# Layer 0's late modulation on TensorE and by row sums, and a z gate that is kept until the scan is done

## The chip, the cores and the metric

The program runs on one core of one Trainium2 chip, as one launch. The metric is the device time of one execution, in microseconds (us). TensorE does the matmuls, VectorE (DVE) and ScalarE (ACT) the elementwise work, GpSimd (POOL) a part of it, and SyncE (SP) issues nearly all DMA transfers, in one queue. Each engine takes its instructions strictly in the order in which they stand.

## The reference

A backbone of two layers works on 128 context tokens and 512 latent tokens, 640 columns in all, with 1024 features. What matters here:

```
mod = silu(c) @ w_ada[l] + b_ada[l]          # (c_ctx for context, c for latent tokens)
shift1, scale1, gate1, shift2, scale2, gate2 = split(mod, 6)
h = rmsnorm(x) * (1 + scale1) + shift1
cq, ckv, krope, dq, dk, dv, z, xbc, dt_raw = split(h @ w_in)
o_a = latent attention(cq, ckv, krope); o_d = differential attention(dq, dk, dv)
y   = scan(xbc, dt_raw)                      # forward and backward, chunks of 128 tokens
o_c = rmsnorm(y * silu(z), ssm_norm_g)
x  += gate1 * (concat(o_a, o_d, o_c) @ w_out)
h   = rmsnorm(x) * (1 + scale2) + shift2
x  += gate2 * (relu(h @ w_ff1)**2 @ w_ff2)
```

Everything is float32. A modulation vector of 1024 numbers for two conditions is a product of a 1024x1024 block of `w_ada` with two vectors. The blocks are numbered j = 0 to 5 in the order of the split: 0 is the first shift, 2 the first gate, 3 the second shift, 4 the second scale.

## The kernel before, in words

Activations lie with features on partitions: `x[k]` holds 128 features of all 640 tokens, for k = 0 to 7. Large products run as three passes over a high and a low part of each operand (`fm`, L318; `tm_chunk`, L781 to L783). The layer's mixing stage (`mixing`, L594) is written as generators: `projections` (the low-rank and query/key projections, then z in `gate`, L795), `ssd` (the scan), `att_b` (differential attention), `prep_a` (keys and queries of the latent attention), `att_a` (latent attention), `wo_part` (output projection). `weave` (L186) steps whichever part is furthest behind its share, and so sets the order in which the program is written; a scheduler then orders each engine's queue by readiness with that order as priority. The first weave ends when the projections are done, the second when the scan is, the third covers the rest of the differential attention, and two more the latent attention.

A part named `fill` carries modulation vectors that are needed later in the layer or in the next one. `pace` (L1673, L1681, L1691) sets its share in each stage from `FILL`, three numbers a layer. Layer 0's fill before is `ada_all` with blocks 2, 3 and 4: `ada_dve` loads 16 pieces of 256 KB of a block and adds them up, each row weighted with the condition's value, in the tile `wc` (VectorE L433; ScalarE L431 and L436; GpSimd L437), and ends with one-column matmuls against ones (`adad`, L414) that sum over partitions. Layer 1's fill is `ada_rows` with blocks 3 and 4: the condition is broadcast to rows once (`crow`, L463), and each piece of the transposed block is multiplied and summed along its row by one VectorE instruction with an accumulator (`junk`, L484). The first gate has to be ready before the output projection begins, so a loop steps the fill nine times there.

In `gate`, z's tile `zth` holds z times 1 + tanh(z/2). Then the generator yields until the scan's output `ys` of its tokens exists, and multiplies it (L813). The scan's `gated` (L1217) waits for both products of a chunk, normalizes it, and its result is transposed (`yT`) for the output projection. `zth` comes from a ring X of 6 buffers; the ring G has 48, the ring Y 13. `PB` is a ring of 3 PSUM banks, from which small products of all parts are taken.

Of the kernel before, what the change touches and what calls it, by code (L numbers as in the profile page):

```python
# [21 lines left out]
P = 128  # L22
# [77 lines left out]
ADA_T = [(0, 5)] + [(1, j) for j in (1, 0, 2, 3, 4, 5)]  # L100
# [4 lines left out]
def build(nc, tc, a, ctx):  # L105
# [291 lines left out]
    def ada_dve(l, j):  # L397

        def fetch(i):
            qr, k2 = divmod(i, 4)  # L400
            raw = Y([P, 2, 256], name="wa")
            nc.sync.dma_start(raw, a["w_ada"][k2 * 256:(k2 + 1) * 256, j * 1024 + qr * 256:j * 1024 + (qr + 1) * 256]
                              .rearrange("(k p) c -> p k c", p=P))
            return raw

        pt = S([P, 8, 2], "adapt", 2)
        raws = [fetch(0), fetch(1)]

        def columns(qr, acc):
            pp = PB("adad")  # L410
            for m in range(2):
                for v in range(2):
                    c = 2 * m + v
                    pe.matmul(pp[:, c:c + 1], acc[:, v, m * P:(m + 1) * P], ones[:, 0:1], start=True, stop=True)  # L414
            act.copy(out=pt[:, qr * 2:qr * 2 + 2], in_=pp[:, :4].rearrange("p (m v) -> p m v", v=2))

        lag = []
        for i in range(16):
            qr, k2 = divmod(i, 4)
            if k2 == 0:  # L420
                if len(lag) == 2:
                    columns(*lag.pop(0))
                acc = Y([P, 2, 256], name="wc")
                lag.append((qr, acc))
            for kk in range(2):
                k = 2 * k2 + kk
                r = raws[i][:, kk]
                for v in range(2):
                    s_ = sc[:, k, v:v + 1]
                    if k == 0:  # L430
                        act.activation(out=acc[:, v], in_=r, func=AF.Copy, scale=s_)  # L431
                    elif v == 0 or k in ADA_DVE[l]:
                        vec.scalar_tensor_tensor(out=acc[:, v], in0=r, scalar=s_, in1=acc[:, v], op0=ALU.mult, op1=ALU.add)  # L433
                    else:
                        t_ = X([P, 256], name="adat")
                        act.activation(out=t_, in_=r, func=AF.Copy, scale=s_)  # L436
                        pool.tensor_tensor(out=acc[:, v], in0=acc[:, v], in1=t_, op=ALU.add)  # L437
            if i + 2 < 16:
                raws.append(fetch(i + 2))
            if i % 2:  # L440
                yield
        for qa in lag:
            columns(*qa)
        ada_finish(l, j, pt)
        yield

    def ada_all(items):
        for l, j in items:
            for _ in ada_dve(l, j):
                mark("fill")  # L450
                yield
                mark("fill")

    def ada_rows(items):
# [19 lines left out]
        for i, (l, j, m, h) in enumerate(units):  # L474
            if m == 0 and h == 0:
                res = S([P, 2, KD, 2], "adares", 2)
            for v in range(2):
                junk = X([P, 512], name="junk")
                sum_ = res[:, h, m, v:v + 1]
                if 2 * h + v in ROWS_POOL:  # L480
                    pool.tensor_tensor(out=junk, in0=raws[i], in1=row[v][h], op=ALU.mult)
                    act.activation(out=junk, in_=junk, func=AF.Copy, accum_out=sum_)
                else:
                    vec.scalar_tensor_tensor(out=junk, in0=raws[i], scalar=1.0, in1=row[v][h], op0=ALU.mult, op1=ALU.mult,  # L484
                                             accum_out=sum_)
            if i + 2 < len(units):
                raws.append(fetch(i + 2))
            if h == 1:
                if m == KD - 1:
                    sm = S([P, 8, 2], "adapt", 2)  # L490
                    vec.tensor_tensor(out=sm, in0=res[:, 0], in1=res[:, 1], op=ALU.add)
                    ada_finish(l, j, sm)
                yield
                mark("fill")

# [98 lines left out]
    def mixing(l, nrm, fill, late=None, raws={}):  # L594
# [196 lines left out]
        ys, gates = [], [0] * NT  # L791
# [3 lines left out]
        def gate(ci, names, n):  # L795
            lab = f"{l}z"
            for tp, ps in tm_chunk(names, n, lab):
                if tp:
                    m = len(tp)
                    th = X([P, 2, 256], name="zth")  # L800
# [7 lines left out]
                    while len(ys) <= tp[-1]:  # L808
                        yield
                    mark(lab)  # L810
                    for i, t in enumerate(tp):
                        yh = ys[t][:, ci * 256:(ci + 1) * 256]
                        vec.scalar_tensor_tensor(out=yh, in0=yh, scalar=0.5, in1=th[:, i], op0=ALU.mult, op1=ALU.mult)  # L813
                        gates[t] += 1
# [167 lines left out]
        def ssd():  # L982
# [234 lines left out]
            def gated(c):  # L1217
                mark(lab)
                y = ys[c]
                sq = X([P, 512], name="ysq")  # L1220
# [27 lines left out]
            for c in range(NT):  # L1248
                while gates[c] < 2:
                    yield  # L1250
# [432 lines left out]
        while l == 0 and fill.k < 9:  # L1683
# [38 lines left out]
    FILL = (.01, 6, 25), (8, .01, 9)  # L1722
    ROWS_POOL = ()
    ADA_DVE = ((1, 4, 7), (1, 4, 7))
# [303 lines left out]
    for l in range(DEPTH):  # L2028
        f0 = Part(ada_all([(0, 2), (0, 3), (0, 4)]) if l == 0 else ada_rows([(1, 3), (1, 4)]), 1)
# [126 lines left out]
```

## Time and profile before

| | us |
|---|---|
| median of 3 runs (1852.67 to 1854.27) | 1853.48 |
| the profiled execution, device time | 1856.54 |
| its span, first to last instruction | 1854.7 |
| TensorE busy in it | 1734.9 |
| VectorE busy | 1361.3 |
| ScalarE busy | 856.2 |
| GpSimd busy | 499.0 |

The mean granted TensorE clock was 0.946 of full speed. The clock has two levels, 1.2 and 2.4 GHz, so a stretch with a granted clock of 0.75 spent half its time at each. A matmul's busy time contains its way through the array and overlaps with the next one's: how fast matmuls follow each other is read from their starts.

A float32 matmul stands in the trace as two records, each with a weight load of its own; one of the kinds that the large products use stands there as one.

### The profile page before, as it was taken

The page shows a single profiled execution, that of the slowest core. Times are in us where ns is not written, and L with a number is a line of the kernel's source. Part 1 is how long each engine was busy: PE and PEld are TensorE (multiplying, and loading weights), DVE is VectorE, ACT ScalarE, POOL GpSimd, SP SyncE. Part 2 cuts the span into 40 slices and gives each one's busy share as a digit, 9 for nine tenths or more (in the row PEclk, how much of TensorE's full clock was granted, in tenths as well). Part 3 has the DMA queues.
Part 4 walks back from the last instruction along what each step waited for, and adds up shares of the span by engine and source line. Part 5 has one row for each costly group of instructions (what it writes and reads, how often), then busy time and mean ns, then how long its engine had stood idle before and what let it go on. Part 6 is the DMA issues. An engine that isn't in the chain of part 4 may idle for free. (4 is left out here: it accounts for less than half of the span.)

```text
span 1854.7 us, 31728 instructions
## 1 busy us (share of the span) xinstructions
PE 1734.9 (94%) x11572; PEld 1636.7 (88%) x11572; DVE 1361.3 (73%) x2843; ACT 856.2 (46%) x1801; POOL 499.0 (27%) x586
## 2 busy tenths in 40 slices
PE   6999985999899999999998998889999999999998
PEld 4798864888899999999998987668998999999998
DVE  6785768866978988686766769878677887465562
ACT  6553355764555351433544533377544545243240
POOL 1444335212430322304144343331103032130400
PEclk8999976997999999999998998789999999999999
DMA  9121122233343437264441322212423342525341
GB/s 333 56 86 42 49 62 83 80 127 107 109 144 110 141 117 244 89 226 132 164 147 50 98 79 64 70 49 74 137 65 117 94 129 74 187 89 162 112 155 56
DMA packets 116589, 209.01 MB, mean 113 GB/s; under 512 B 13392, under 2 KB 28624, under 8 KB 116432
## 3 DMA queue, kind: packets, MB, share of 16 engines
q1 hardware_dynamic: 115872, 206.80, 34.7%
q8 instruction: 91, 1.49, 0.3%
q14 instruction: 66, 0.54, 0.1%
q10 hardware_dynamic: 560, 0.18, 0.0%
HBM read 179.51 MB, written 27.43 MB: 112 GB/s over the span
## 5 line engine op out<-in xcount | busy, mean ns | idle before, releaser
L1801 ACT CAST wh<-wr 128x512 fp32r<-128x512 f32 x232 | 143.7, 620 | 302.3 <-PE fm L1831 198.0
L1831 PE MATMUL fm<-ul,wh 128*128 128x320 f32 x1024 | 235.2, 311 | 10.2 <-DVE ul L307 10.2
L1802 DVE TENSOR_TENSOR wl<-wr,wh 128x512 fp32r<-128x512 f32 x232 | 180.1, 785 | 77.0 <-issue 41.6
L1831 PE MATMUL fm<-uh,wh 128*128 128x320 f32 x1024 | 234.4, 310 | 1.3 <-DVE x L562 1.3
L1831 PE MATMUL fm<-uh,wl 128*128 128x320 f32 x1024 | 234.5, 310 | 0.0
L1788 POOL TENSOR_TENSOR wS<-wr,wr 128x512 f32<-128x512 f32 x48 | 78.5, 1634 | 494.8 <-DMA wr<-in_W 213.2
L1831 PEld LDWEIGHTS fm<-ul,wh 128*128 128x128 f32 x1024 | 172.1, 189 | 11.3 <-DVE ul L307 11.3
L1831 PEld LDWEIGHTS fm<-uh,wh 128*128 128x128 f32 x1024 | 172.4, 189 | 1.7 <-ACT wh L1801 1.5
L1831 PEld LDWEIGHTS fm<-uh,wl 128*128 128x128 f32 x1024 | 172.7, 189 | 0.0
L484 DVE SCALAR_TENSOR_TENSOR junk<-wa,crow 128x512 f32<-128x512 f32 x224 | 154.0, 735 | 8.4 <-DMA wa<-in_w_adaT 8.2
L562 DVE SCALAR_TENSOR_TENSOR x<-fm,mod,x 128x128 f32<-128x128 f32 (+2 forms) x192 | 72.6, 433 | 108.6 <-PE fm L1831 108.6
L1801 ACT CAST wh<-wS 128x512 fp32r<-128x512 f32 x96 | 59.7, 622 | 142.9 <-PE fm L1831 68.9
L782 PE MATMUL tm<-wl,hhi 128*128 128x256 f32 (+2 forms) x400 | 120.4, 301 | 4.1 <-POOL wl L297 2.0
L781 PE MATMUL tm<-wh,hhi 128*128 128x256 f32 (+2 forms) x400 | 121.2, 303 | 2.5 <-DVE zth L802 1.9
L783 PE MATMUL tm<-wh,hlo 128*128 128x256 f32 (+2 forms) x400 | 120.2, 301 | 0.0
L296 ACT CAST wh<-wr 128x512 fp32r<-128x512 f32 (+2 forms) x108 | 66.5, 625 | 74.8 <-PE fm L318 30.5
L1831 PE MATMUL ffx<-eh,wh 128*128 128x320 f32 x288 | 89.3, 310 | 0.0
L1831 PE MATMUL ffx<-el,wh 128*128 128x320 f32 x288 | 89.2, 310 | 0.0
L1831 PE MATMUL ffx<-eh,wl 128*128 128x320 f32 x288 | 89.1, 309 | 0.0
L782 PEld LDWEIGHTS tm<-wl,hhi 128*128 128x128 f32 x400 | 81.1, 203 | 5.5 <-DVE wl L297 2.7
L781 PEld LDWEIGHTS tm<-wh,hhi 128*128 128x128 f32 x400 | 81.1, 203 | 4.8 <-DVE zth L802 2.6
L783 PEld LDWEIGHTS tm<-wh,hlo 128*128 128x128 f32 x400 | 81.1, 203 | 0.6
(390 smaller groups left out, 4875.8 us busy)
## 6 DMA issues: line engine op xcount, KB each, us to landing
wr<-in_W SPq DMA_DIRECT2D x351, 256.0 KB, 2.8
wa<-in_w_adaT SPq DMA_DIRECT2D x112, 256.0 KB, 4.2
xsave<-x SPq DMA_DIRECT2D x72, 320.0 KB, 2.2
x<-xsave SPq DMA_DIRECT2D x72, 320.0 KB, 5.0
wa<-in_w_ada SPq DMA_DIRECT2D x48, 256.0 KB, 3.6
war<-in_w_ada SPq DMA_DIRECT2D x32, 256.0 KB, 5.3
x<-in_xT SPq DMA_DIRECT2D x16, 320.0 KB, 4.7
out_yT<-x SPq DMA_DIRECT2D x8, 320.0 KB, 2.2
```

The lines of the kernel that those rows point to most:

```text
L296: act.copy(out=hi[:, :w], in_=raw[:, :w])
L484: vec.scalar_tensor_tensor(out=junk, in0=raws[i], scalar=1.0, in1=row[v][h], op0=ALU.mult, op1=ALU.mult, accum_out=sum_)
L562: vec.scalar_tensor_tensor(out=x[m][:, t0:t0 + n], in0=src, scalar=mods[l][:, j, m, v:v + 1], in1=x[m][:, t0:t0 + n], op0=ALU.mult, op1=AL ...
L781: pe.matmul(ps[:, i, :n], hh[k][:, ts], hi[:, c:c + n], start=s, stop=False)
L782: pe.matmul(ps[:, i, :n], hh[k][:, ts], lo[:, c:c + n], start=False, stop=False)
L783: pe.matmul(ps[:, i, :n], hl[k][:, ts], hi[:, c:c + n], start=False, stop=e)
L1788: pool.tensor_tensor(out=box[key], in0=box[x0], in1=box[x1], op=op)
L1801: act.copy(out=hi, in_=raw)
L1802: vec.tensor_tensor(out=lo, in0=raw, in1=f(hi), op=ALU.subtract)
L1831: mm = pe.matmul(o, w_, x_[:, ts], start=s_, stop=e_, skip_group_check=on)
```

## The change

Layer 0's blocks 2 and 3 are made by a new `ada_pe`: for each 128 outputs, a 1024x128 strip of `w_ada` is loaded in two pieces of 256 KB (512 bytes in a row), and eight float32 matmuls of 128x2 accumulate the result directly, with the weights stationary and the condition's two columns moving. Block 4 is made by `ada_rows`, from a transposed copy that is added to the inputs. `FILL` of layer 0 changes, and the loop before the output projection steps the fill until the first gate is made. The z tiles come from the ring G and are kept in a list; `gate` no longer yields for the scan, and `gated` does the products.

```diff
-ADA_T = [(0, 5)] + [(1, j) for j in (1, 0, 2, 3, 4, 5)]
+ADA_T = [(0, 4), (0, 5)] + [(1, j) for j in (1, 0, 2, 3, 4, 5)]
...
+    def ada_pe(l, j):
+
+        def fetch(m):
+            raw = [Y([P, 4, P], name="wa") for _ in range(2)]
+            for h in range(2):
+                c = j * 1024 + m * P
+                nc.sync.dma_start(raw[h], a["w_ada"][h * 512:(h + 1) * 512, c:c + P].rearrange("(k p) c -> p k c", p=P))
+            return raw
+
+        raws = [fetch(0)]
+        res = S([P, KD, 2], "adapt", 2)
+        for m in range(KD):
+            mark("fill")
+            if m + 1 < KD:
+                raws.append(fetch(m + 1))
+            ps = PB("adap")
+            for k in range(KD):
+                pe.matmul(ps[:, 0:2], raws[m][k // 4][:, k % 4], sc[:, k], start=(k == 0), stop=(k == KD - 1))
+            act.copy(out=res[:, m], in_=ps[:, 0:2])
+            if m == KD - 1:
+                ada_finish(l, j, res)
+            yield
+
+    gates_made = []
+
+    def ada_first():
+
+        for m, _ in enumerate(ada_pe(0, 2)):
+            if m == KD - 1:
+                gates_made.append(0)
+            yield
+        yield from ada_pe(0, 3)
+        yield from ada_rows([(0, 4)])
...
-        ys, gates = [], [0] * NT
+        ys, gates = [], [[] for _ in range(NT)]
...
-                    th = X([P, 2, 256], name="zth")
+                    th = G([P, 2, 256], name="zth")
...
-                    while len(ys) <= tp[-1]:
-                        yield
-                    mark(lab)
                     for i, t in enumerate(tp):
-                        yh = ys[t][:, ci * 256:(ci + 1) * 256]
-                        vec.scalar_tensor_tensor(out=yh, in0=yh, scalar=0.5, in1=th[:, i], op0=ALU.mult, op1=ALU.mult)
-                        gates[t] += 1
+                        gates[t].append(th[:, i])
...
             def gated(c):
                 mark(lab)
                 y = ys[c]
+                for ci in range(2):
+                    yh = y[:, ci * 256:(ci + 1) * 256]
+                    vec.scalar_tensor_tensor(out=yh, in0=yh, scalar=0.5, in1=gates[c][ci], op0=ALU.mult, op1=ALU.mult)
...
-                while gates[c] < 2:
+                while len(gates[c]) < 2:
...
-        while l == 0 and fill.k < 9:
+        while not gates_made:
             fill.step()
...
-    FILL = (.01, 6, 25), (8, .01, 9)
+    FILL = (2, 20, 9), (8, .01, 9)
...
-        f0 = Part(ada_all([(0, 2), (0, 3), (0, 4)]) if l == 0 else ada_rows([(1, 3), (1, 4)]), 1)
+        f0 = Part(ada_first() if l == 0 else ada_rows([(1, 3), (1, 4)]), 1)
```

On TensorE, in layer 0's differential attention, before: `stkT` stacks queries and keys, `scB` are scores, `adad` sums `wc` over partitions, `wo` is the output projection.

```order
L318 MATMUL wo_772_3422<-mCl_2864,wh_2834 128x320
L318 MATMUL wo_772_3422<-mCh_2860,wl_2835 128x320
L922 MATMUL stkT_3222<-identr,box_3195 96x128
L414 MATMUL adad_3278<-masksr,wc_3076 128x1
L922 MATMUL stkT_3222<-identr,box_3195 96x128 x3
L1567 MATMUL scB_3399<-stk_3227,stk_3205 128x256
L1567 MATMUL scB_3403<-stk_3227,stk_3205 128x256
L414 MATMUL adad_3278<-masksr,wc_3076 128x1 x3
L414 MATMUL adad_3317<-masksr,wc_3245 128x1 x4
L414 MATMUL adad_3352<-masksr,wc_3284 128x1 x4
```

And now, some fifty rows earlier in the same stage; `kva` are the latent attention's keys and values, and `adap` reads two loaded pieces `wa`:

```order
L1542 MATMUL scB_2966<-stk_2855,stk_2867 128x128
L1303 MATMUL kva_2977<-wukv_2913,ckc_2919 128x512
L456 MATMUL adap_2988<-sc,wa_2634 128x2 x4
L456 MATMUL adap_2988<-sc,wa_2635 128x2 x4
L1303 MATMUL kva_3024<-wukv_2913,cqf_1935 128x512
L1542 MATMUL scB_3033<-stk_2879,stk_2891 128x256
L1542 MATMUL scB_3033<-stk_2901,stk_2891 128x256
L1542 MATMUL scB_3033<-stk_2855,stk_2891 128x128
```

The matmuls that waited for VectorE's sums are gone, and groups of eight that need loaded weights alone stand between the scores from the stage's head on: two such steps lie in the projections before it and fourteen in this stage.

On VectorE, where layer 0's projections end and the differential attention begins (`box` prepares the stacks, `xtm` is the scan's output), before:

```order
L813 SCALAR_TENSOR_TENSOR xtm_1515<-xtm_1515,zth_2791 128x256
L813 SCALAR_TENSOR_TENSOR xtm_1581<-xtm_1581,zth_2791 128x256
L297 TENSOR_TENSOR wl_3810<-wr_3807,wh_3809 128x512
L297 TENSOR_TENSOR wl_4057<-wr_4054,wh_4056 128x512
L1224 TENSOR_SCALAR yvv_2800<-yss_2798 128x1
L1224 TENSOR_SCALAR yvv_2808<-yss_2806 128x1
L802 SCALAR_TENSOR_TENSOR zth_2844<-zth_2844,tm_2813 128x256
L813 SCALAR_TENSOR_TENSOR xtm_1650<-xtm_1650,zth_2844 128x256
L914 TENSOR_TENSOR box_2865<-dxr_2072,box_2865 128x2x32
```

And now:

```order
L1155 TENSOR_TENSOR eg_2740<-eg_2740,cbm_2627 128x512
L886 TENSOR_TENSOR box_2845<-dxr_1455,box_2845 128x2x32 x2
L886 TENSOR_TENSOR box_2857<-dxr_2179,box_2857 128x2x32 x2
L886 TENSOR_TENSOR box_2869<-dxr_1560,box_2869 128x2x32 x2
L1172 TENSOR_TENSOR xtm_1650<-yd_2779,xD_2823 128x512
L886 TENSOR_TENSOR box_2881<-dxr_2283,box_2881 128x2x32
L1186 TENSOR_TENSOR xtm_1650<-xtm_1650,yo_2829 128x256
L1186 TENSOR_TENSOR xtm_1650<-xtm_1650,yo_2836 128x256
```

The end of the scan and the products with z now lie among the first `box` operations instead of ahead of them.

## Rows read from the trace of the kernel before

**Rows 1.** The page: busy time, and the clock in 40 slices.

```profile
PE 1734.9 (94%) x11572; PEld 1636.7 (88%) x11572; DVE 1361.3 (73%) x2843; ACT 856.2 (46%) x1801; POOL 499.0 (27%) x586
...
PEclk8999976997999999999998998789999999999999
```

**Rows 2.** Windows: stretch, length, busy us of PE, PEld, DVE, ACT, POOL, clock, DMA.

```profile
161.00:260.00 99.00, 94.06 (x571) 77.67 (x569) 71.82 (x147) 36.43 (x89) 35.41 (x32) 0.88 0.13 38
...
298.00:325.00 27.00, 15.69 (x80) 14.32 (x80) 22.09 (x46) 11.22 (x29) 12.14 (x17) 0.56 0.24 74
325.00:389.00 64.00, 60.85 (x459) 56.14 (x457) 54.64 (x158) 44.67 (x105) 16.15 (x34) 1.00 0.28 91
389.00:515.00 126.00, 114.44 (x811) 110.17 (x810) 91.42 (x196) 68.78 (x163) 41.80 (x43) 0.89 0.35 112
1089.00:1202.00 113.00, 99.61 (x573) 82.24 (x572) 92.73 (x206) 36.71 (x90) 38.04 (x34) 0.82 0.22 68
1202.00:1240.00 38.00, 30.14 (x157) 23.21 (x157) 27.71 (x80) 27.72 (x68) 14.66 (x36) 0.82 0.11 37
1240.00:1305.00 65.00, 63.40 (x469) 58.23 (x469) 55.98 (x163) 45.71 (x108) 12.84 (x28) 1.00 0.27 86
1305.00:1404.00 99.00, 92.70 (x743) 89.93 (x741) 72.53 (x172) 51.34 (x112) 16.87 (x22) 1.00 0.27 87
```

**Rows 3.** Windows, instructions on tile wc alone, columns as in rows 2.

```profile
260.00:298.00 38.00, 1.35 (x7) 1.32 (x7) 8.11 (x15) 2.70 (x6) 5.77 (x6) 0.68 0.31 99
298.00:325.00 27.00, 6.04 (x26) 5.80 (x26) 15.30 (x26) 0.91 (x2) 8.60 (x10) 0.56 0.24 74
...
389.00:515.00 126.00, 8.77 (x64) 8.85 (x64) 40.19 (x80) 7.25 (x16) 27.65 (x32) 0.89 0.35 112
```

**Rows 4.** Windows, instructions on tile junk alone: DVE busy, clock, DMA.

```profile
1089.00:1202.00 113.00, 22.56 (x56) 0.82 0.22 68
...
1305.00:1404.00 99.00, 18.09 (x56) 1.00 0.27 87
```

**Rows 5.** TensorE's waits (us in total, times, longest): 260:330, then 1089:1205.

```profile
PE adad L414 <- DVE wc L433: 12.5, 3, 8.8
PE stkT L922 <- DVE box L914: 6.9, 3, 3.4
...
PE stkT L922 <- DVE box L914: 5.8, 2, 5.3
...
PE tm L781 <- DVE zth L802: 1.9, 1, 1.9
```

**Rows 6.** Groups by line: count, busy us, mean ns, idle time before and its releaser.

```profile
L484 DVE SCALAR_TENSOR_TENSOR junk<-wa,crow 128x512 f32<-128x512 f32 x224 | 154.0, 735 | 8.4 <-DMA wa<-in_w_adaT 8.2
L433 DVE SCALAR_TENSOR_TENSOR wc<-wa,sc,wc 128x256 f32<-128x256 f32 x120 | 63.6, 566 | 8.7 <-ACT wc L431 7.3 <-POOL wc L437 1.2
L484 DVE DVE_READ_ACCUMULATOR junk<-wa,crow 128x1 f32 x224 | 18.2, 81 | 0.0
L463 PE MATMUL crow<-identr,sc 128*128 128x128 f32 x96 | 11.8, 276 | 0.0
L813 DVE SCALAR_TENSOR_TENSOR xtm<-xtm,zth 128x256 f32<-128x256 f32 x20 | 8.1, 418 | 0.1
```

**Rows 7.** Timeline of TensorE: start, us, line, operation, tiles, records.

```profile
80.89 2.73 PE L700 MATMUL bshp<-mod,wr 128*128 128x2 f32 x24
83.49 0.37 PE L781 MATMUL tm<-wh,hhi 128*128 128x272 f32 x1
```

**Rows 8.** Windows up to and behind cqss, then behind bshp, columns as in rows 2.

```profile
161.20:168.00 6.80, 6.80 (x62) 6.80 (x60) 5.28 (x13) 1.61 (x4) 0.00 (x0) 1.00 0.15 45
168.00:174.80 6.80, 6.80 (x24) 5.17 (x24) 2.12 (x6) 1.19 (x2) 2.99 (x2) 0.50 0.00 0
...
83.50:90.00 6.50, 6.50 (x54) 6.50 (x54) 6.50 (x7) 0.66 (x2) 1.81 (x5) 1.00 0.42 123
```

**Rows 9.** Tile wa from 270 to 520: its DMAs.

```profile
DMA to landing us min/median/max: 2.5/3.3/7.2
```

More of the change, by code (lines that the diff above doesn't have):

```diff
@@ L395, in half @@
             ada_finish(self.l, self.j, sm, slice(4 * h, 4 * h + 4))
[L397 to L440, printed above, removed]
-                yield
[L442 to L452, printed above, removed]
     def ada_rows(items):
@@ L807, in gate @@
                             nc.sync.dma_start(a["o_kr"][l], krope[:, 0])
-                    while len(ys) <= tp[-1]:
-                        yield
-                    mark(lab)
                     for i, t in enumerate(tp):
-                        yh = ys[t][:, ci * 256:(ci + 1) * 256]
-                        vec.scalar_tensor_tensor(out=yh, in0=yh, scalar=0.5, in1=th[:, i], op0=ALU.mult, op1=ALU.mult)
-                        gates[t] += 1
+                        gates[t].append(th[:, i])
                 yield
@@ L1721, in build @@
     AP1, AP0 = (1, 4), ()
-    FILL = (.01, 6, 25), (8, .01, 9)
+    FILL = (2, 20, 9), (8, .01, 9)
     ROWS_POOL = ()
-    ADA_DVE = ((1, 4, 7), (1, 4, 7))
     CONV_POOL = ()
```

## The prediction, made before the change was run

> **What bounds the kernel now.** I read the page's busy shares first: TensorE is busy for 94% of the span and nothing else comes near it [rows 1]. But the page's clock row falls to 6 and 7 tenths in slices near 280 and 1180 us [rows 1], so I cut both layers' attention into three stages and asked for the windows. In both layers P is the projections beside the scan (161 to 260, 1089 to 1202), B the differential attention (260 to 389, 1202 to 1305), A the latent attention with the rest of the output projection (389 to 515, 1305 to 1404) [rows 2]. The two layers do the same attention work, and yet B takes 129 us in layer 0 against 103 in layer 1, and A 126 against 99. The windows of the tile `wc` say what layer 0 has and layer 1 hasn't: the weighted sums of the modulation cost VectorE 23.4 us inside B (8.11 and 15.30, all before 325) and 40.2 us inside A [rows 3]. Layer 1 instead spends its row sums in P (22.6 us) and A (18.1 us) and none in B [rows 4]. The waits name the price: between 260 and 330 TensorE stands 12.5 us before the `adad` matmuls until a `wc` is done, one wait of 8.8 us [rows 5], and from 298 to 325 its clock is granted at 0.56, with 15.7 of 27 us busy [rows 2]. So layer 1 is my model of a layer 0 without that work, and I add what the change puts in its place.
>
> **The change, part by part.**
>
> *The gate and second shift go to TensorE.* Removed with the second scale's sums: 120 VectorE operations of 566 ns, 63.6 us [rows 6], with their ScalarE and GpSimd partners, and 48 tiny matmuls. Added: 16 steps, each two loads of 256 KB, eight float32 matmuls of 128x2 and one small copy. Their form stands in the trace already: `bshp` is a 128x128 float32 weight with two moving columns, and 12 of them (24 records) run from 80.89 to 83.49, 0.217 us each [rows 7]. A step is thus 8 x 0.217 = 1.7 us at 2.4 GHz and 16 steps are 28 us; at 1.2 GHz it is twice that. The order puts two steps in P, fourteen in B and none in A. Of B's fourteen, five stand ahead of the first `pT`, in the stretch that layer 1 has from 1202 to 1240. There TensorE is busy 30.1 of 38 us at a clock of 0.82 [rows 2], waiting on VectorE and ScalarE, so five steps (8.7 us) about fit in its 7.9 us of idle time. I cost them at nothing; they cost 8.7 us if the gaps lie elsewhere. The other nine meet a TensorE that is busy 63.4 of 65 us and cost 9 x 1.73 = 15.6 us in full.
>
> *A clock term.* Matmuls with one or two columns keep the engine busy, but rows show the clock dropping behind them: behind the one-column run of `cqss` it is 0.50 from 168.0 to 174.8, though TensorE was busy without a gap at 1.00 before; behind the `bshp` run it stays at 1.00 [rows 8]. A fall costs half its length, 1.7 to 3.4 us. Runs in the change are shorter (1.7 us against the 2.6 of `bshp`) and lie between other work, so I take two falls, 4 us; none is 0, one behind each of the nine steps is 9 x 2.5 = 22 us.
> By the Trainium skill (TensorE: Matmul & The Clock Gate, The HAM clock gate) the clock follows how busy the engine has been and drops after idleness. By that rule these runs would cost no fall and the time would be 4 us less; the `cqss` rows disagree.
> By the Trainium skill (FP8 and Floating Point Precision, on FP32 in the PE array) a true float32 product takes four passes. If so, and each pass cost what a record does here, a step would take twice as long and the 28 us added would be 55, which undoes the gain. The trace decides against it for this form: 24 records for 12 matmuls, two each.
>
> *The matmuls wait for their own weights.* `adap` stands in TensorE's queue, and what is behind it (`kva`, `scB`) waits too, and behind that VectorE's maxima. From issue to landing a `wa` took 2.5 to 7.2 us, median 3.3 [rows 9]. The new loads have the same bytes in pieces half as long, which no row shows: from 2.5 to 7.2 us, and I take 3.3. They are issued one step ahead, so most arrive in time; the first has only 17 matmuls of cover (about 2 us), so 1.3 us shows, and I add nothing for the rest. If every step waited 3.3 us it would be 53 us.
>
> *The second scale by row sums.* 32 operations of 735 + 81 ns = 26 us on VectorE [rows 6], all in A and early there; layer 1's A holds 18.1 us of the same with VectorE busy 72.5 of 99 [rows 2, 4]. The row broadcast adds 16 matmuls and their share of the 11.8 us that 48 take, 3.9 us [rows 6].
>
> *z no longer waits.* Directly it waited for little: the only wait of `tm` on `zth` is 1.9 us [rows 5]. What moves is work: ten products per layer (half of 8.1 us, 4 us [rows 6]) leave P for the head of B, where they stand before the transposes of the scan's output, so the output projection starts later; 24 of its matmuls pass from B to A in both layers, which cancels. And the matmuls of z, left over behind the scan before, now lie between its waits. P ends before with an idle TensorE until a `box` comes, 5.8 us in layer 1 [rows 5].
>
> *Layer 1's row sums.* With fewer turns taken by the projections, two of its steps (8 x 0.816 = 6.5 us of VectorE) go from P to the end of A. P has VectorE busy 92.7 of 113 us, so it gains; at the end of A the second norm waits for these sums.
>
> **The sum**, against the profiled run's 1856.5 us. Layer 0: P: +3.5 (two steps) +1.3, less 4.8, my share of the 6.9 us that `stkT` waits for `box` at B's head [rows 5] and that z's matmuls and the scan's end can fill: 0 (bounds -6 to +6). B: 103 from layer 1, + 4 moved products + 15.6 + 4 = 126.6 against 129, -2 (-20 if all steps hide and no clock falls, +20 if none hides and it falls each time). A: 99 + 3.9 = 103 against 126, -23 (-27 to -14, if the sums bind as late ones do). Layer 1: P -6 (0 to -12), B +4 (0 to +4), A +3 (half of 6.5; 0 to +6.5): +1. Together -24, 1832.5; the median of the runs lies 3.1 us under the profiled one, so **1830 us**. What is late next in B is TensorE itself.
>
> **The rivals.**
> 1. *The small matmuls are paid twice.* In B no step hides (+8.7) and the clock falls behind each dense step (22 instead of 4): 1830 + 27 = 1857 if all of it, about 1846 at half. For it: the `cqss` rows. Against: `bshp`.
> 2. *TensorE waits on the loads (slower).* Place: the steps of B, whose tiles come free late; SyncE issues in order. Price: up to 3.3 us a step, 53 us, 1883; half of it 1856. It decides from 24 / 16 = 1.5 us per step. Against: the order leaves 40 or more matmuls between most loads and their use, some 5 us.
> 3. *More is won.* All steps of B fit in its waits and no clock falls: B is 107, -20, 1810.
> 4. *The sums were not the cause in A.* If layer 0's A is long for another reason, only its `adad` go: about 1850. Against: its idle time and low clock lie where `wc` runs.
> That z's rewrite does nothing by itself is inside the forecast.
>
> **Chances.** Forecast 0.55 (1815 to 1843); rival 1 0.15, rival 2 0.10, rival 3 0.12, rival 4 0.08. The range 1812 to 1848 leaves out half of rival 3 below and rival 2 with the upper parts of 1 and 4. A measurement here tells 0.2% (3.7 us) from no change. Faster takes the forecast, rival 3 and over half of 1 and 4: 0.81; the same 0.07; slower 0.12.
>
> **What would show it.** Right: layer 0's A within 100 to 108 us at a clock near 1.0; B at 118 to 132 us with `adap` waits under 8 us in sum and no `wc`; layer 1's stages each within 8 us of before. Wrong: B over 135 us, a clock under 0.9 in its second half (rival 1), or `adap` waiting on loads for over 20 us (rival 2); A above 115 us (rival 4).

## The result, and the profile after

The changed kernel took 1844.1 us (median of 6 runs, 1838.0 to 1845.4) against 1853.1 us of the kernel before: a ratio of 0.9946, 95% interval 0.9924 to 0.9967. It is faster, by 9 us. The forecast was 1830 us, a gain of 24 us, so it had the side right and the size wrong by more than half.

The page of the changed kernel, the rows that answer to [rows 1]:

```profile
PE 1752.6 (95%) x11764; PEld 1659.3 (90%) x11764; DVE 1330.3 (72%) x2788; ACT 828.8 (45%) x1737; POOL 464.5 (25%) x538
...
PEclk8899866899999999999999999889999999999999
```

VectorE, ScalarE and GpSimd have less to do, as the change meant. TensorE has 18 us more, and the dip of the clock near 280 us is still there (8, 6, 6 where there were 7, 6); the dip of layer 1 is shallower.

The windows of the changed kernel by stage, columns as in [rows 2]. Layer 0 first (P from 161 to the first `stkT`, B to the first `scA`, A to the end of the output projection), then layer 1:

```profile
161.00:272.00 111.00, 105.94 (x602) 87.35 (x600) 71.81 (x137) 32.01 (x78) 39.38 (x35) 0.81 0.18 53
272.00:403.00 131.00, 128.98 (x825) 117.42 (x826) 89.51 (x256) 80.75 (x203) 31.51 (x67) 0.80 0.34 103
403.00:512.00 109.00, 102.24 (x803) 99.28 (x803) 73.79 (x181) 54.10 (x115) 14.46 (x19) 0.98 0.28 92
1089.00:1185.00 96.00, 86.61 (x575) 72.74 (x573) 85.98 (x174) 32.13 (x77) 41.22 (x33) 0.97 0.24 73
1185.00:1286.00 101.00, 93.42 (x604) 81.40 (x604) 87.08 (x254) 76.23 (x184) 31.48 (x64) 0.86 0.18 57
1286.00:1393.00 107.00, 100.81 (x770) 97.86 (x768) 80.95 (x198) 52.92 (x116) 16.04 (x23) 0.95 0.32 102
```

Against [rows 2], layer 0's P is 12 us longer, B 2 us longer and A 17 us shorter; layer 1's P is 17 us shorter, B 2 us shorter and A 8 us longer. Layer 0 as a whole won nothing in this execution (its feed-forward begins at 643.4 us, before at 643.6), and the 13 us between the two spans lie behind it: 11 of them in layer 1's three stages, for which I had forecast +1.

In B the reader is to compare busy time with length. Before, B holds 104 us of TensorE in 129:

```profile
260.10:389.20 129.10, 104.07 (x652) 91.21 (x652) 106.55 (x283) 84.97 (x204) 46.90 (x85) 0.81 0.28 89
```

Now it holds 129 in 131. The waits are gone, and work stands in their place. TensorE's waits of the changed kernel from 161 to 403 us (in total, times, longest) answer to [rows 5]:

```profile
PE stkT L894 <- DVE box L886: 2.5, 1, 2.5
PE seg L1146 <- POOL acmov L1067: 1.7, 1, 1.7
PE kva L1303 <- DMA wukv<-in_W: 1.2, 1, 1.2
```

The 12.5 us before `adad` are gone, and no `adap` waits for its weights. But the work runs slowly. The windows of the changed kernel where the clock is lowest:

```profile
247.00:305.00 58.00, 54.09 (x200) 43.84 (x199) 36.75 (x89) 28.51 (x71) 20.84 (x40) 0.50 0.26 72
```

For 58 us TensorE is busy nearly throughout and is granted 0.50, its level of 1.2 GHz. By the Trainium skill (TensorE: Matmul & The Clock Gate, The HAM clock gate) the clock is set by how busy the engine has been; 54 of 58 us busy, as the profile counts it, at half clock disagree, as the `cqss` rows did [rows 8].

A measure for the rest of the text: a stretch of length L at a mean clock c loses L x (1 - c) to the clock, known to about 1 us, as c has two digits. It counts time at half clock in which TensorE had nothing to do as well: of the 47.8 us at half clock in B before, TensorE was busy in 32.9, of the 53.6 us now in 52.1. By the windows from each layer's first `tm` to its first `stkT`, then B, then A, with a second execution whose TensorE order in layer 0 is the same (the pacing of layer 1's row sums differs, see `b_l1_6` and `a_l1_10` below):

| layer 0, us (of it lost to the clock) | before | `b_l1_6` | changed | `a_l1_10` |
|---|---|---|---|---|
| first tm to first stkT | 176.6 (12.4) | 182.7 (16.4) | 188.9 (22.7) | 182.3 (12.8) |
| B | 129.1 (24.5) | 128.3 (23.1) | 130.8 (27.5) | 126.9 (21.6) |
| A | 125.6 (13.8) | 120.4 (10.8) | 109.6 (2.2) | 111.1 (3.3) |
| from there to the first ffx | 128.9 | 128.7 | 131.0 | 131.7 |

The two executions of one order differ by up to 7 us in a stage (6.1 us with the old kernel and 6.6 with the new in the first, 0.8 and 3.9 in B, 5.2 and 1.5 in A), most of it clock, so a single profile settles no term under that. Over both, layer 0 won 4 us: P +6, B 0, A -12.6, the rest +2.5.

### The profile page after: what moved, and what is told of

It reads as the page before. It is cut to its first block, busy times and chain, and to the rows that moved or that the text cites. A ratio compares the mean times of both kernels' runs of the same rounds, so it can differ in the third digit from the quotient of the medians.

```text
span 1841.2 us, 31851 instructions
## 1 busy us (share of the span) xinstructions
PE 1752.6 (95%) x11764; PEld 1659.3 (90%) x11764; DVE 1330.3 (72%) x2788; ACT 828.8 (45%) x1737; POOL 464.5 (25%) x538
## 5 line engine op out<-in xcount | busy, mean ns | idle before, releaser
L427 DVE SCALAR_TENSOR_TENSOR junk<-wa,crow 128x512 f32<-128x512 f32 x256 | 176.7, 739 | 7.4 <-DMA wa<-in_w_adaT 5.7
L539 DVE SCALAR_TENSOR_TENSOR x<-wo,mod,x 128x128 f32<-128x128 f32 (+1 forms) x144 | 57.0, 432 | 39.0 <-PE wo L318 38.5
```

What stands on the lines that cost most here:

```text
L539: vec.scalar_tensor_tensor(out=x[m][:, t0:t0 + n], in0=src, scalar=mods[l][:, j, m, v:v + 1], in1=x[m][:, t0:t0 + n], op0=ALU.mult, op1=AL ...
```

## The experiments

Each was timed in five rounds beside the kernel before, which by these runs took 1850.8 to 1853.1 us. Lost to the clock here is the whole span times one less its mean clock, the median over the runs.

| kernel | median us | ratio to before, 95% interval | lost to the clock |
|---|---|---|---|
| before | 1850.8 to 1853.1 | 1 | 98 |
| changed | 1844.1 | 0.9946 (0.9924 to 0.9967) | 93 |
| `z_only` | 1851.2 | 0.9991 (0.9973 to 1.0009) | 98 |
| `ada_only` | 1862.0 | 1.0059 (1.0040 to 1.0078) | 104 |
| `p_clear` | 1847.1 | 0.9967 (0.9949 to 0.9985) | 91 |
| `one_quarter` | 1821.8 | 0.9836 (0.9808 to 0.9865) | 82 |
| `primed` | 1843.3 | 0.9967 (0.9949 to 0.9986) | 91 |
| `primed_wide` | 1841.4 | 0.9952 (0.9936 to 0.9969) | 70 |
| `p8` | 1851.3 | 1.0001 (0.9978 to 1.0024) | 98 |
| `keeper` | 1840.2 | 0.9947 (0.9926 to 0.9967) | 74 |
| `before_warm` | 1856.4 | 1.0026 (1.0008 to 1.0044) | 92 |
| `keep_stk` | 1842.4 | 0.9957 (0.9941 to 0.9974) | 67 |
| `all_warm` | 1855.2 | 1.0018 (0.9998 to 1.0038) | 72 |
| `clear_keep` | 1850.8 | 1.0017 (0.9991 to 1.0042) | 85 |
| `b_l1_6` | 1849.3 | 0.9988 (0.9972 to 1.0004) | 98 |
| `a_l1_10` | 1847.2 | 0.9978 (0.9958 to 0.9998) | 97 |
| `keeper_l5` | 1844.8 | 0.9972 (0.9950 to 0.9994) | 76 |

### The two halves of the change apart

`z_only` is the kernel before with z's part of the diff; `ada_only` the changed kernel with that part undone:

```diff
-                    while len(ys) <= tp[-1]:
-                        yield
...
-                        vec.scalar_tensor_tensor(out=yh, in0=yh, scalar=0.5, in1=th[:, i], op0=ALU.mult, op1=ALU.mult)
+                        gates[t].append(th[:, i])
```

> The kernel before with only z's rewrite (its gates kept in long-lived tiles, the products beside the transposes); layer 0's modulation stays as it was. Theory 1 (the clock): layer 1's 13 us are z's, and layer 0's projections end 12 us later in the changed kernel because narrow matmuls of the new modulation hold the clock at 0.50, so without them layer 0 keeps its 260 us to the first stkT and 389 to the first scA: layer 1 gains 13 us, 1840 us. Theory 2 (z itself): z's matmuls no longer lie between waits and that is what makes layer 0's projections longer: first stkT of layer 0 near 270, layer 1 gains 13, 1850 us.

> The changed kernel with z as it was before (its projection yields until the scan's output is there); layer 0's modulation by TensorE and by row sums, layer 0's new pacing. Theory 1 (the clock): layer 0 gains 0 to 4 us by the end of its output projection, layer 1 stays within 4 us of before: 1849 to 1853 us. Theory 2 (z itself costs layer 0 its 12 us): layer 0 gains 14 to 20 us and layer 1 nothing: 1833 to 1839 us.

The modulation alone made the kernel slower by 0.6%, z alone changed nothing that the measurement tells, and both together gained 0.5%. Neither theory had the sum. By the stages: in `z_only` layer 0's first `stkT` came at 254.0 us, which refutes the second theory (270), though that one had the whole time (1850). In `ada_only` it came at 275.7, so the late end of P belongs to the modulation, with or without z. Layer 1's stretch from the first `tm` to the first `stkT` took 188.2 us in `z_only` and 204.1 in `ada_only`, against 199.0 before. Two effects that add would give a ratio of 0.9991 x 1.0059 = 1.0050 where 0.9946 was measured. The order of TensorE's instructions in layer 1 is not excluded as a cause: by the traces, 62 of the 1134 records from the first `tm` to the first `stkT` stand elsewhere in the changed kernel than in `z_only`, and 21 of 1142 there and 109 of 620 in B elsewhere in `ada_only` than before. But kernels with one and the same order in layer 1 differ there as well (the last group comes back to it), so this 1% stays open.

### What the small matmuls cost

`one_quarter` does two of each step's eight products and leaves the other six out of the gate and the shift:

```diff
-            for k in range(KD):
-                pe.matmul(ps[:, 0:2], raws[m][k // 4][:, k % 4], sc[:, k], start=(k == 0), stop=(k == KD - 1))
+            for k in (0, 4):
+                pe.matmul(ps[:, 0:2], raws[m][k // 4][:, k % 4], sc[:, k], start=(k == 0), stop=(k == 4))
```

> The changed kernel with two of the eight matmuls of each adap step (the products of k = 0 and 4; the other six are left out of the gate and the shift): the same loads, copies and order. Theory 1 (TensorE is what layer 0 waits for, at half clock): 96 of 128 adap matmuls go, 0.23 us each at 2.4 GHz and 0.43 at 1.2: 22 to 41 us less, 1805 to 1822 us. Theory 3 (loads or VectorE's work set the pace of layer 0's B, TensorE only looks busy): less than 8 us, 1837 to 1844 us.

It ran 22.3 us faster than the changed kernel (1821.8 against 1844.1), for 96 matmuls that start 0.224 us apart at 2.4 GHz, 21.5 us of work. The theory that loads or VectorE set the pace is out. The window of layer 0's B in `one_quarter`:

```profile
267.00:376.00 109.00, 99.08 (x667) 88.23 (x668) 87.53 (x254) 79.55 (x202) 32.32 (x67) 0.88 0.41 124
```

From here to the changed kernel's B (131 us, 129.0 busy, 0.80) there are 14 x 6 matmuls more, 18.8 us at full clock. Busy time grows by 29.9 us, 1.6 times that, because the clock falls from 0.88 to 0.80; 8 us of it lie in time in which TensorE waited (9.9 us in `one_quarter`, 2.0 in the changed kernel), and B grows by 22. So both of what I had weighed against each other happens: some steps hide, and B as a whole pays more than their price, 22 us for 18.8. No stage shows the steps alone, since the order of other matmuls moved with them: A is 6 us longer in `one_quarter`, and up to the feed-forward (624.8 against 643.4 us) the two executions differ by 18.6 us for 21.5 us of matmuls. By the whole kernel's medians 96 matmuls are worth 22.3 us, give or take some 7 by the two intervals, which is about their price; scaled to all 128, an estimate, 22.3 x 128 / 96 = 29.7 us.

### Whether the late first load delays the scan

In the changed kernel the first step's loads are issued with the step. The build puts the step back in TensorE's order until they are expected, with the scan's head behind it, and 93 more of z's `tm` matmuls go ahead: 333 of 600 stand before the first `cqss`, where 240 did. `primed` issues the loads ahead of the projections and has 240 again; `p_clear` has no step in P; `p8` has eight.

```diff
+        if prime:
+            yield                # in ada_pe, behind the first two loads
...
+        if l == 0:
+            fill.step()          # primed: only the first two loads
         pace(fills[0])
...
-    FILL = (2, 20, 9), (8, .01, 9)
+    FILL = (.01, 20, 9), (8, .01, 9)      # p_clear; p8: (9, 20, 9) with primed's loads
```

> The changed kernel with layer 0's pacing (.01, 20, 9) in place of (2, 20, 9): no adap step beside the projections, all 16 behind them. Theory 1, in its strict form (the step at 243.5 sets off the fall at 247.2): the clock falls of layer 0's projections are those of before (24 us at 0.50 against 42), the first stkT comes at 258 to 262 instead of 272, and the two steps cost 3.7 us later: 1835 to 1840 us. Theory 1b (any dense row of narrow matmuls makes it fall, with or without adap): first stkT at 266 to 270, 3.7 us given back later: 1843 to 1845 us.

> The changed kernel with the first two adap loads issued ahead of the projections instead of with the first step. In the changed kernel's order 333 of the 600 tm matmuls of layer 0 stand ahead of the scan's first cqss, in the kernel before and here 240. Theory 4 (the order): because its loads come late, the first adap step and the scan's head behind it are put back, z's wide matmuls go ahead, and the rest of the scan then runs without them at half clock. Then cqss starts at 164 to 168 us, the first stkT at 258 to 263 (256.4 without any step there, plus 3.7), half clock before it 8 to 25 us instead of 45: 1832 to 1838 us. Theory 1 (the adap steps themselves make the clock fall there): first stkT 268 to 272, half clock 35 to 45 us, 1842 to 1846 us.

> As the one with early loads, with layer 0's pacing (9, 20, 9): eight adap steps beside the projections instead of two, eight behind. Theory 1 (the steps cost 3.4 us each in B at half clock and 1.84 among z's wide matmuls at full clock): P longer by 6 x 1.84 = 11 us, B shorter by 14 to 20, 3 to 9 us less than with two. Rival (every step costs its 1.84 us wherever it stands): the same time within 3 us. Rival (they hold the scan up as the late load did): P longer by over 18 us, slower.

`primed` brought `cqss` from 175.1 to 165.9 us as expected, but the first `stkT` only to 265.1, and its whole time, 0.9967 of before, is not below the changed kernel's 0.9946. In `a_l1_10`, with the changed kernel's order, `cqss` came at 175.6 and `stkT` still at 266.2. So the scan's late start is real, and that it costs the 12 us is not shown. `p_clear` has its first `stkT` at 256.4 and gives it back: B 137.1 us (all 16 steps) and A 120.0. `p8` moves them the other way, P 194.3, B 134.8, A 100.9, and is slower; its B is longer with six steps fewer, but about two thirds of block 4's 32 row sums (14.2 us of VectorE) now stand in it, so it does not price the steps alone. Moving steps between the stages moves the time with them.

The windows from layer 0's first `tm` to its first `stkT`, in before, `z_only`, `p_clear`, `primed` and the changed kernel:

```profile
83.50:260.10 176.60, 171.48 (x1113) 147.99 (x1112) 130.00 (x259) 73.81 (x174) 66.42 (x76) 0.93 0.19 57
83.70:254.00 170.30, 166.14 (x1103) 144.24 (x1103) 128.06 (x246) 69.06 (x161) 66.77 (x75) 0.98 0.20 59
84.50:256.40 171.90, 167.70 (x1105) 145.81 (x1104) 126.08 (x246) 69.34 (x161) 65.52 (x74) 0.97 0.20 57
83.30:265.10 181.80, 177.42 (x1144) 155.07 (x1144) 127.99 (x255) 69.40 (x163) 67.05 (x76) 0.93 0.21 60
83.10:272.00 188.90, 183.74 (x1136) 158.19 (x1135) 128.50 (x249) 69.16 (x163) 68.38 (x76) 0.88 0.21 61
```

With the new z and no step beside it the stretch is 5 to 12 us shorter than with the old z (176.6 in before, 182.7 in `b_l1_6`), and two steps beside it take that back and more, most of it by the clock: 178 to 189 us over seven kernels.

### What the clock would give

`keeper` puts useless work ahead of every step: three matmuls of 128x512 on constants, whose result the step overwrites. `primed_wide` turns each product round, so that 128 columns of `w_ada` move through two columns of weights. Both have `primed`'s early loads.

```diff
             ps = PB("adap")
+            for _ in range(3):
+                pe.matmul(ps, identr, masksr[:, 0:4].rearrange("p a b -> p (a b)"), start=True, stop=True)
...
-                pe.matmul(ps[:, 0:2], raws[m][k // 4][:, k % 4], sc[:, k], ...)          # primed_wide:
+                pe.matmul(ps[:2, 0:P], sc[:, k], raws[m][k // 4][:, k % 4], ...)
```

> As the one with early loads, and ahead of each adap step three matmuls of 128x512 on constants, whose result is overwritten: 48 more wide matmuls, about 0.22 us each at 2.4 GHz, 10.5 us of TensorE. Theory 1 (the clock in B follows how many columns TensorE streams, not how busy it is): half clock in B falls from 54 us to under 35, and B is no longer than 131 us although 9 us were added: 1830 to 1838 us. Rival (more work is more time): half clock unchanged, B 140 to 146, 10 to 15 us slower than without them.

> As the one with early loads, and each adap product turned round: the two columns of the modulation's input are the weight and 128 columns of w_ada move through, with one 2x128 transpose a step (a step later). The same loads and products. Theory 1 (few moving columns hold the clock at 0.50 in B): half clock in layer 0's B falls from 54 us to under 30, B from 131 to 112 to 120 us, 1818 to 1828 us. Rival (the attention's own narrow matmuls keep it down, whatever the adap steps stream): half clock stays at 45 to 58 us, B 128 to 134, 1832 to 1845 us.

Windows of layer 0's B in `primed`, then in `keeper`, then in `primed_wide`:

```profile
265.10:393.30 128.20, 127.17 (x819) 115.73 (x818) 87.96 (x248) 80.77 (x202) 30.98 (x67) 0.80 0.35 105
```

```profile
265.30:390.10 124.80, 121.09 (x824) 108.22 (x825) 85.97 (x247) 79.79 (x200) 32.53 (x67) 0.89 0.33 98
```

```profile
258.80:390.00 131.20, 122.31 (x833) 99.01 (x834) 89.69 (x257) 83.22 (x215) 31.77 (x69) 0.91 0.33 98
```

The 48 added matmuls start 0.234 us apart at 2.4 GHz, 11.2 us of TensorE. The kernel with them takes no longer (1840.2 against 1843.3 us for `primed`, intervals overlapping): in B the clock rises from 0.80 to 0.89, and the time at half clock falls from 51 to 27 us. B is 3 us shorter, but one of its fourteen steps and 12 `wo` matmuls have passed on to A, which is 3 us longer (`primed`, then `keeper`):

```profile
393.30:504.90 111.60, 104.12 (x806) 100.95 (x805) 74.67 (x182) 54.51 (x116) 14.89 (x20) 0.97 0.28 90
390.10:504.90 114.80, 107.39 (x840) 104.12 (x839) 76.54 (x188) 55.69 (x119) 14.83 (x20) 0.99 0.30 98
```

B and A together take 239.6 us against 239.8, with 42 of the added matmuls (9.8 us) in them. So with wide matmuls among the narrow ones the clock rose, as the theory said. What it hoped for is not there: what the clock gives back pays for the added matmuls. `primed_wide` has the clock too (24 us at half), at the same price a step (its records start 0.109 us apart, the narrow ones 0.112), and its B, with one step less and 12 `wo` matmuls more, is no shorter: TensorE now waits 9 us there, 3.8 of it for `box`. By these waits the attention's own chain is late next.

Three more mixes of the same: `keep_stk` adds one constant matmul to each `stkT` group, `all_warm` one to each `seg` as well, `clear_keep` is `p_clear`'s pacing, at 24, with the constant matmuls.

```diff
                             pt = PB("stkT")
+                            pe.matmul(pt, identr, masksr[:, 0:4].rearrange("p a b -> p (a b)"), start=True, stop=True)
...
                     psg = PB("seg")          # all_warm, and before_warm below
+                    pe.matmul(psg, identr, masksr[:, 0:4].rearrange("p a b -> p (a b)"), start=True, stop=True)
...
-    FILL = (2, 20, 9), (8, .01, 9)
+    FILL = (.01, 24, 9), (8, .01, 9)      # clear_keep
```

> The kernel with early loads and three constant 128x512 matmuls ahead of each adap step, and one more ahead of each stkT group in both layers (22 a layer, 0.23 us each at 2.4 GHz). Theory 1: layer 1's B, at 0.50 for 28 of its 101 us in every kernel with the new z, falls under 20 us of it and to 95 to 100 us; layer 0's B stays within 3 us of 125: 1832 to 1839 us. Rival (the head of B waits for boxes and copies, the clock is not what it lacks): layer 1's B 101 to 106 us, 1841 to 1850 us.

> As the one with constant matmuls ahead of adap steps and stkT groups, and also ahead of each seg accumulation of the scan in both layers (20 a layer). Theory 1: the projections of both layers lose what they still have at 0.50 (20 us in layer 0, 16 in layer 1, half of it is 18 us) and pay 9.4 us for it: 1826 to 1836 us. Rival (past the first third the added work costs more than the clock gives): 1838 to 1846 us.

> The changed kernel with pacing (.01, 24, 9), so no adap step beside layer 0's projections, and three constant 128x512 matmuls ahead of each step. Theory 1: P as without steps there (171 to 173 us), B with all 16 steps and 48 constant matmuls but half clock under 35 us (129 to 135 us), A near 115: layer 0 552 to 556 us from its first tm to its first ffx, 1834 to 1841 us. Rival (the steps' work is the same wherever it stands and only A grows, as without the constant matmuls: 120 us): 557 us or more, 1842 to 1848 us.

Theory 1 missed in all three. `keep_stk` lost 7 us less to the clock than `keeper` and took no less time (1842.4 us, in the rival's range); layer 1's B grew from 101.2 to 110.5 us, beyond even the rival, with the clock at the same 0.86:

```profile
1176.60:1287.10 110.50, 101.12 (x639) 86.93 (x637) 94.39 (x267) 77.62 (x187) 35.35 (x72) 0.86 0.18 57
```

Its projections are 4 us shorter for it (180.6 against 184.6 us): work passed from one stage to the next, and the 5.3 us that both together grew are about the price of the 22 added matmuls (5.1 us at 0.234). `all_warm` was 15 us slower than `keeper`, beyond both ranges: its matmuls cost more than the clock returned. `clear_keep` took the 555.7 us in layer 0 that theory 1 gave it, but with 47.8 us at half clock in B instead of under 35, and its whole time is beyond both ranges.

### What z's part won in layer 1

`before_warm` adds one constant matmul ahead of each `seg` of the scan (the edit shown above) to the kernel before. `b_l1_6` is the kernel before with eight of layer 1's row sums moved out of its projections, `a_l1_10` the changed kernel with eight moved back in, `keeper_l5` is `keeper` with eight more moved out:

```diff
-    FILL = (.01, 6, 25), (8, .01, 9)
+    FILL = (.01, 6, 25), (6, .01, 9)      # b_l1_6
...
-    FILL = (2, 20, 9), (8, .01, 9)
+    FILL = (2, 20, 9), (10, .01, 9)       # a_l1_10; keeper_l5: 5
```

> The kernel before, with one matmul of 128x512 on constants ahead of each seg accumulation of the scan, its result overwritten: 20 in each layer, 0.23 us each at 2.4 GHz, 4.7 us of TensorE a layer. Nothing else is changed: z waits as before and the modulation is as before. Theory 1 (what z's rewrite won in layer 1's projections is clock: over the kernels so far their length is 177.5 us plus half of the time at 0.50): half clock there falls from 44 us to under 30, and the stretch from layer 1's first tm to its first stkT shrinks from 199 to 189 to 196 us although work is added; 1843 to 1850 us in all. Rival (z's gain is its freed TensorE time and VectorE order): half clock stays at 40 to 50 and both layers get 4 to 6 us longer, 1859 to 1863 us.

> The kernel before with layer 1's row sums paced 6 instead of 8: 28 of them beside its projections instead of 36, as in the changed kernel; the other eight come later. Theory 5 (VectorE's chain through the scan bounds layer 1's projections): eight sums of 0.82 us less there, from the first tm to the first stkT 190 to 194 us instead of 199, with the wait of stkT for box gone or under 3 us. Theory 1 (the clock): the stretch stays at 196 to 201 us and follows its half clock (44 us before). Whole kernel: 1845 to 1849 or 1850 to 1854 us.

> The changed kernel with layer 1's row sums paced 10 instead of 8: 36 of them beside its projections as in the kernel before, instead of 28. Theory 5 (VectorE's chain): from the first tm to the first stkT of layer 1 187 to 190 us instead of 182, whatever the clock, A 4 to 7 us shorter. Theory 1 (the clock): 178 us plus half of the time at 0.50, which no count of row sums sets.

> The kernel with early loads and three constant 128x512 matmuls ahead of each adap step, with layer 1's row sums paced 5: 20 of them beside its projections, the rest later. Theory 5: layer 1's projections 5 to 7 us shorter than with 28 (184.6 us), A within 4 us of 106.5: 1834 to 1838 us. Theory 1: no shorter, 1840 us; longer if the late sums bind at the end of A, 1842 to 1848 us.

Layer 1 from its first `tm` to its first `stkT`, in the kernels with the old z and in those with the new:

| kernel | length, us | lost to the clock | length less that |
|---|---|---|---|
| before | 199.0 | 21.9 | 177.1 |
| `ada_only` | 204.1 | 24.5 | 179.6 |
| `b_l1_6` | 196.9 | 21.7 | 175.2 |
| `before_warm` | 198.6 | 13.9 | 184.7 |
| changed | 182.0 | 5.5 | 176.5 |
| `z_only` | 188.2 | 9.4 | 178.8 |
| `primed` | 190.7 | 13.3 | 177.4 |
| `keeper` | 184.6 | 7.4 | 177.2 |
| `keeper_l5` | 184.9 | 7.4 | 177.5 |
| `a_l1_10` | 194.7 | 13.6 | 181.1 |

The windows of before, the changed kernel and `primed`:

```profile
1002.90:1201.90 199.00, 182.84 (x1143) 157.60 (x1143) 154.65 (x331) 75.79 (x178) 73.62 (x88) 0.89 0.25 76
1003.10:1185.10 182.00, 167.81 (x1134) 146.53 (x1135) 147.69 (x298) 70.67 (x164) 78.10 (x86) 0.97 0.25 77
997.60:1188.30 190.70, 175.82 (x1135) 152.95 (x1135) 144.81 (x299) 70.79 (x164) 76.37 (x87) 0.93 0.25 74
```

Without added work every length is 175 to 181 us plus what the clock lost, and the new z loses 5 to 14 us where the old one loses 22 to 25. The row sums are not it: taking eight out of the old kernel changed 2 us, and `keeper_l5` won nothing; putting eight in cost 2 to 5 us beside the clock. `before_warm` is the test that the clock theory failed: it got back 8 us of clock, and the stretch did not shrink. Its wait list for that stretch says where they went:

```profile
PE stkT L922 <- DVE box L914: 9.2, 1, 9.2
```

That wait was 5.3 us before [rows 5]: the scan's last boxes come no sooner here for a faster TensorE, and the added matmuls cost 4.7 us. The test is not a clean one, since with the added matmuls 186 of the stretch's other 1142 records stand elsewhere in the order. So with the new z the time at half clock is less and the stretch shorter by as much; that is shown. That raising the clock by itself would give it is not shown, and why the stretch's loss is 5 in one kernel and 13 in another with the same TensorE order (the changed kernel and `primed`) is open.

## Why the prediction was wrong

Point by point, in the prediction's own steps, with the two executions of the table above:

- **What bounds the kernel.** Right. The `wc` waits were there and went, and TensorE is what layer 0 waits for (`one_quarter`). But what was to be won in B was the 25 us in which TensorE did not work, and the change brought about as much work.
- **Five steps in B hide, the clock falls twice, P's two cost nothing.** That some hide was right (8 us). The clock term was not: I took 4 us for two falls, and `one_quarter` against the changed kernel shows 11 us in B alone (29.9 busy for 18.8 of work). About half of it falls on the steps themselves: three of the sixteen (282 to 301 us) ran at half clock, where their records start 0.213 us apart instead of 0.112, some 5 us in all; twelve ran at full clock. I priced the 16 steps at 19.6 us net; about 30 were paid, by the estimate from `one_quarter`. My reading that two records a matmul decide against four passes does not hold: a record of `primed_wide` with 128 moving columns takes 0.109 us from start to start, nearly as long as one of the large products with 256 (0.118), so records are no count of passes. Nothing hung on it, as the 0.217 us were measured whole.
- **P of layer 0: 0 (-6 to +6).** It came out at +12.3 in the profiled execution and at 0 to +6 between the others. Of the 12.3, 10.3 are clock. The 0 was a sum of terms that were too small: the new z won 5 to 12 us, where I had 4.8 from a wait, and the two steps, priced at 3.5, cost 6 to 19 (`z_only`, `p_clear` and `clear_keep` against the kernels with two steps). I had seen that the first step's loads come late and priced it at 1.3 us; that they move the scan's head behind 93 of z's matmuls stood in the order, and I missed it, though no run shows what that costs.
- **B of layer 0: -2.** +1.7 and -1.4: right as a sum, by terms that offset each other. The steps' clock cost more than I took; 24 `wo` matmuls that left B for A (3.5 us at 0.147 from start to start) made up for it, and so did most of the 4 us for moved products: eight of layer 0's ten still stand in P, and the two in B take VectorE 1.0 us. By the prediction's own terms B's bounds are -22 and +24, not -20 and +20.
- **A of layer 0: -23 (-27 to -14).** -16 in the profiled execution, -12.6 over both: the largest mis-sized term. I took layer 1's A of the kernel before as the base (99 us, nothing lost to the clock) and let the 24 `wo` matmuls that come over from B cancel. In A they are paid: 99.2 + 3.5 + 3.6 for `crow` (32 records at 0.112) + 2.2 to 3.3 that the clock still loses is 108.5 to 109.6, and 109.6 and 111.1 were measured. The other part is the start: A of the kernel before took 125.6 us in the execution I read and 120.4 in another. Behind A 2.5 us were lost that I had at nothing.
- **Layer 1: +1.** -11 in the profiled executions: P -17, B -1.5 and A +7.3, where I had -6, +4 and +3. Over the experiments that leave layer 1's part as it is, its three stages take 389 to 399 us with the new z, 401 and 407 with the old. I took z's rewrite as moved work and priced its waits (1.9 us). What it changed was how long TensorE ran at half clock beside the scan, 16.4 of P's 17 us; the row sums, from which I had P's -6, are worth some 2 us (`b_l1_6`).
- **The rivals.** Rival 1 (paid twice, 1846 at half its price) comes nearest: the time, the clock in B's second half (0.88 from 315 to 403 us) and B's busy time, which grew by 1.6 times the price of the matmuls; that no step hides was wrong in it. Rival 2 is out, no `adap` waited. Rival 4 is half right: A is longer than the model for the `wo` matmuls, though not for an unknown cause.
- **The base.** The profiled run of before (span 1854.7 us) lies at the slow end: 115 runs had a median span of 1850.2.

The step that failed is "layer 1 is my model of a layer 0 without that work", and with it P's 0. The model gave A 103 us, -23; 109.6 and 111.1 were measured, -12.6 over both pairs of executions, because the `wo` matmuls that I let cancel are paid there and A before was no more than 120.4 in its second execution. P, for which I had 0, came to +6 over both pairs and +12.3 in the profiled one, 10.3 of that clock. The model took the waits and the low clock of layer 0 as the price of `wc`. The waits were; the low clock of B was not: TensorE was busy at half clock for 32.9 us of B before and for 52.1 after. The attention runs at half clock without any modulation beside it, too: 28 us of layer 1's B in the changed kernel. So layer 0 won 4 us over both pairs, and nothing in the profiled executions. That the kernel came out faster by 9 us rests in good part on layer 1, which the sum had at +1: the side was right partly by luck, and the cause of that gain stays open.

## What to carry to other kernels

When work moves from a late engine to the one that is already busy for 94%, price it in full at the busy engine and let only the measured idle time of that very stretch pay for it; another layer's stretch is a model only if the same instructions stand in it, so count them on both sides. Read the order for what a late load pushes behind it, not only for the wait itself. Where the clock moves with the mix of matmuls, expect a few us of scatter in any stage of one profile and compare medians, or a second execution of the same order.

## What the runs showed of the hardware that I had not expected

- Runs of one and the same program differ by their clock. Of 115 runs of the kernel before, the 11 with a mean granted clock of 0.943 to 0.944 had a median span of 1854.4 us, the 37 with 0.949 or more 1847.0 us; the spread, 1843.0 to 1859.9 us, is of the size of the effect that was to be measured.
- 48 matmuls whose result nobody reads cost nothing that the measurement tells: `keeper` has 11.2 us more TensorE work than `primed`, lost 17 us less to the clock (74 against 91), and took 1840.2 us against 1843.3.
- At 2.4 GHz a float32 matmul with 128x128 weights and two moving columns takes as long (two records, 0.112 us apart: 0.22 us) as one with two columns of weights and 128 moving (two records, 0.109 us apart: 0.22 us).
